# Squares of an RMS norm added in pairs on VectorE ahead of the matmuls that sum them over partitions

## The chip, the cores and the metric

The kernel runs on the 8 cores of one Trainium2 chip. The time of a run is that of its slowest core, in microseconds (us) of the device. A run can fall into a slow state, in which the cores of one die show a lower granted TensorE clock. Unless said otherwise, a time is the median over all runs of a kernel, slow ones included, as the timing reports it; where that matters, the fast runs alone are given beside it.

TensorE (PE) multiplies matrices; its weight loads (PEld) overlap with it (in the second profile of the kernel before, 1898.4 and 875.3 us busy in a span of 2054.5 us). VectorE is DVE, ScalarE is ACT, GpSimd is POOL. The order of instructions on each engine is written down when the program is built.

## The reference, cut to what matters

A decoder step: retention layer, then sliding-window attention layer, each followed by a SwiGLU feed-forward network (FFN), for a prompt (8 sequences of 2048 tokens) and a sample group (128 sequences of 8 tokens). The width is 1024. What the change touches is the norm alone:

```python
def rms_norm(x, g):
    xf = x.astype(jnp.float32)
    y = xf * lax.rsqrt(jnp.mean(xf * xf, axis=-1, keepdims=True) + RMS_EPS)
    return (y * g.astype(jnp.float32)).astype(x.dtype)

for layer in range(DEPTH):          # cut
    hp = rms_norm(xp, norm_mix[layer]);  hs = rms_norm(xs, norm_mix[layer])
    ...                             # retention or attention
    xp = xp + yp;  xs = xs + ys
    xp = xp + swiglu(rms_norm(xp, norm_ffn[layer]), ...)
    xs = xs + swiglu(rms_norm(xs, norm_ffn[layer]), ...)
y_prompt = rms_norm(xp, norm_final);  y_sample = rms_norm(xs, norm_final)
```

## The kernel before: the parts that matter

The activations lie with the 1024 channels on partitions, as `KC = 8` tiles ("columns") of 128 partitions by 512 tokens (prompt) or 128 tokens (sample). The sum over the channels is therefore a sum over partitions and over the eight columns. ScalarE squares each column into one of six buffers `sq`, and TensorE multiplies a matrix of ones by it, eight matmuls that accumulate into one PSUM bank. A core does 25 such norms, 20 of 512 columns (large) and 5 of 128 (sample): 200 matmuls on squares.

```python
def norm_do_sq(self, j):
    kc = j.sq.pop(0)
    s = self.sqi % 6
    while s in self.sqown:
        self.norm_do_mm(self.sqown[s])
    self.sqi += 1
    cx = j.cx
    self.act(self.sq[:, s, :cx.NT], cx.x[:, kc, :cx.NT], AF.Square, [cx.xb[kc]], [self.sqb[s]])
    j.mm.append(s)
    self.sqown[s] = j

def norm_do_mm(self, j):
    ...                                   # cut: takes a PSUM bank
    s = j.mm.pop(0)
    del self.sqown[s]
    NT = j.cx.NT
    self.mm(j.bk[:, :NT], self.cb[:, CB_ONES:CB_ONES + 128], self.sq[:, s, :NT],
            j.nmm == 0, j.nmm == KC - 1, [self.sqb[s], self.cbb], [j.bb])
    j.nmm += 1
    ...                                   # cut: after the eighth, 1/rms on ScalarE
```

When these go into the static order of instructions is decided at build time. After each piece of other work (8 to 16 matmuls, say) the norms get a turn, and a matmul on squares is placed as soon as the scheduler's own clock says that its square is done:

```python
def norm_tick(self):
    t = self.S.t["pe"] + 0.05             # the scheduler's clock for TensorE
    for j in list(self.jobs):
        if j.out:
            self.norm_do_out(j, 2)        # VectorE: two columns of h = x * g / rms
            continue
        for _ in range(4):
            if j.sq and self.S.t_read(j.cx.xb[j.sq[0]]) <= t + 0.5:
                self.norm_do_sq(j)
        while j.mm and self.S.t_read(self.sqb[j.mm[0]]) <= t:
            self.norm_do_mm(j)

def mm(self, out, lhsT, rhs, start, stop, r, w, skip=False):   # its model of a matmul
    k = 0.5 if lhsT.shape[0] <= 64 or self.n(lhsT) <= 64 else 1.0
    self.S.op("pe", ..., dur=k * max(0.1, self.n(out) * 0.00047))
```

The softmax here doesn't subtract the row's maximum and nothing guards it: scores larger than these inputs give would overflow.

Of the kernel before, what the change touches and what calls it, by code (L numbers as in the profile page):

```python
# [9 lines left out]
ALU = mybir.AluOpType  # L10
# [3 lines left out]
KC = 8  # L14
# [373 lines left out]
CB_ONES = 128  # L388
# [120 lines left out]
class Kern:  # L509
# [150 lines left out]
    def norm_begin(self, cx, gi, pool, to_x=False, after=None):  # L660

        j = Ctx()
        j.cx, j.gi, j.pool, j.to_x, j.after = cx, gi, pool, to_x, after
        j.sq, j.mm, j.nmm, j.out, j.bk = [], [], 0, None, None
        self.jobs.append(j)
        cx.job = j
        return j
# [7 lines left out]
# [5 lines that stand above are left out]
        self.sqi += 1  # L680
        cx = j.cx
        self.act(self.sq[:, s, :cx.NT], cx.x[:, kc, :cx.NT], AF.Square, [cx.xb[kc]], [self.sqb[s]])
        j.mm.append(s)
        self.sqown[s] = j

    def norm_do_mm(self, j):
        if j.bk is None:
            pool = j.pool if any(i not in self.held for i in j.pool) else (0, 1, 2, 3)
            j.bk, j.bb, j.hold = self.pb(pool, True)
        s = j.mm.pop(0)  # L690
        del self.sqown[s]
        NT = j.cx.NT
        self.mm(j.bk[:, :NT], self.cb[:, CB_ONES:CB_ONES + 128], self.sq[:, s, :NT], j.nmm == 0, j.nmm == KC - 1, [self.sqb[s], self.cbb], [j.bb])
        j.nmm += 1
        if j.nmm == KC:
            self.nrstd += 1
            j.rstd_ap, (j.rstd_buf,) = self.rstd[self.nrstd % 2]
            for o in list(self.jobs):
                if o.out and o.rstd_buf is j.rstd_buf:
                    self.norm_do_out(o, KC)  # L700
            self.act(j.rstd_ap[:, :NT], j.bk[:, :NT], AF.Ln, [j.bb], [j.rstd_buf], bias=EPS, scale=1.0 / D)
            self.held.discard(j.hold)
            self.act(j.rstd_ap[:, :NT], j.rstd_ap[:, :NT], AF.Exp, [j.rstd_buf], [j.rstd_buf], scale=-0.5)
            j.out = list(range(KC))
# [14 lines left out]
    def norm_tick(self):  # L719

        t = self.S.t["pe"] + 0.05
        for j in list(self.jobs):
            if j.out:
                self.norm_do_out(j, 2)
                continue
            for _ in range(4):
                if j.sq and self.S.t_read(j.cx.xb[j.sq[0]]) <= t + 0.5:
                    self.norm_do_sq(j)
            while j.mm and self.S.t_read(self.sqb[j.mm[0]]) <= t:
                self.norm_do_mm(j)  # L730

    def norm_now(self, cx):

        j = getattr(cx, "job", None)
        if j is None:
            return
        assert j.out or j.nmm + len(j.mm) + len(j.sq) == KC
        while not j.out:
            if j.sq:
                self.norm_do_sq(j)  # L740
                if len(j.mm) < 4 and j.sq:
                    continue
            if j.mm:
                self.norm_do_mm(j)
        self.norm_do_out(j, KC)
# [1139 lines left out]
```

## Time and profile before

| | before |
|---|---|
| time, median of 4 runs | 2054.69 us (2053.55 to 2056.62) |
| span of the profiled cores | 2038.7 to 2058.2 us |
| TensorE busy | 92% |
| VectorE / ScalarE busy | 42% / 36% |
| TensorE waiting for squares | 47.8 us in 39 waits |

The page of the kernel before: part 1 (busy us, share of the span, instructions of each engine), part 4 (the chain that ended last, by engine) and the group of the squares-matmuls in part 5 (busy us, mean ns of one, then the idle time of TensorE just before them).

```profile
PE 1884.1 (92%) x10330; PEld 875.0 (43%) x10514; DVE 870.7 (42%) x1510; ACT 735.0 (36%) x1160; POOL 172.1 (8%) x363
...
PE 75%; DVE 8%; DMA 7%; issue 5%; ACT 4%; DVEq 0%; SPq 0%; POOL 0%; ACTq 0%; another core or an unknown queue 0%; POOLq 0%
...
L576 PE MATMUL ps<-sq,cbt 128*128 128x512 bf16 (+1 forms) x193 | 65.4, 371 | 49.3 <-ACT sq L592 42.9
```

TensorE is what bounds the kernel: it is busy for 92% of the span, and 75% of the chain that ended last lies on it. PE shows 10330 matmuls but 10514 weight loads, so 184 matmul records are missing from this core's trace.

The waits of the kernel before on the same core (engine and what it waited for; us in total, times, longest). One of them, 16.0 us, is at the start of the program, where the first input is loaded.

```profile
PE ps L576 <- ACT sq L592: 47.8, 39, 16.0
```

The timeline of the kernel before in an FFN down-projection (start us, duration us, engine, line, operation, output from inputs, count). Eleven matmuls and one squares-matmul repeat every 2.59 us (2026.04 to 2028.63), so a 128x512 matmul costs 2.59/12 = 0.216 us of the stream, although one alone lasts 0.38 us in the records.

```profile
2023.67 2.54 PE L576 MATMUL ps<-aT_104,wr 128*128 128x512 bf16 x10
2026.04 0.38 PE L576 MATMUL ps<-sq,cbt 128*128 128x512 bf16 x1
2026.26 2.54 PE L576 MATMUL ps<-aT_104,wr 128*128 128x512 bf16 x11
2028.63 0.38 PE L576 MATMUL ps<-sq,cbt 128*128 128x512 bf16 x1
```

And the same view in the second retention stage, where the sample's output projection (4 x 4 matmuls of 128 columns) rides along with the prompt's. In brackets stand TensorE's idle time and what ended it. TensorE's waits for a square stand at the squares-matmuls. (The 0.93 us in the first line stands at an ordinary matmul because the record of the squares-matmul ahead of it is one of the missing ones; its weight load is in the trace, at 1317.48.)

```profile
1317.73 3.61 PE L576 MATMUL ps<-uT_91_134,wr 128*128 128x512 bf16 x16 [0.93 <-ACT sq L592]
1321.18 0.22 PE L576 MATMUL ps<-sq,cbt 128*128 128x128 bf16 x1
1321.24 0.39 PE L576 MATMUL ps<-uTs_121,wr 128*128 128x128 bf16 x4
...
1321.91 0.39 PE L576 MATMUL ps<-uTs_133,wr 128*128 128x128 bf16 x4
1323.12 0.38 PE L576 MATMUL ps<-sq,cbt 128*128 128x512 bf16 x1 [0.83 <-ACT sq L592]
1323.34 3.40 PE L576 MATMUL ps<-uT_91_134,wr 128*128 128x512 bf16 x15
...
1328.73 0.38 PE L576 MATMUL ps<-sq,cbt 128*128 128x512 bf16 x1 [0.83 <-ACT sq L592]
```

### The profile page before, as it was taken

The numbers are of one execution on the slowest core, as the hardware profiler recorded it, in microseconds if no ns is written. First come the engines' busy times: TensorE is split into PE (matmuls) and PEld (weight loads), VectorE is DVE, ScalarE is ACT, GpSimd is POOL, SyncE is SP. The second block draws the span as 40 slices with busy tenths as digits, with TensorE's granted clock in tenths as the row PEclk, the third lists the DMA queues.
The fourth block names the chain that finished last, engine by engine and source line by source line (L and its number), as shares of the span: only waits on it lengthen the run. The fifth ranks groups of instructions, "written<-read, shape, count | busy, mean of one in ns | idle before, by whom it ended". The sixth has DMA issues, their size and how long they took to land.

```text
span 2058.2 us, 30114 instructions; the slowest of 8 cores (2038.7 to 2058.2 us)
## 1 busy us (share of the span) xinstructions
PE 1884.1 (92%) x10330; PEld 875.0 (43%) x10514; DVE 870.7 (42%) x1510; ACT 735.0 (36%) x1160; POOL 172.1 (8%) x363
## 2 busy tenths in 40 slices
PE   4899999999999989899989999899999988899997
PEld 1444444343334334343434444445454532455553
DVE  2454543434335863433555554332222457422224
ACT  2545543321225752122445554221012466310112
POOL 0011111000101000000001111010000000010000
PEclk9899999999999999999999999999999998999999
DMA  9324444897986339888634333554334230134242
GB/s 188 53 40 71 62 72 71 192 192 186 194 183 156 52 63 203 202 204 218 142 113 94 83 72 62 107 82 69 53 57 82 43 62 1 31 66 84 46 73 93
DMA packets 87253, 211.93 MB, mean 103 GB/s; under 512 B 10784, under 2 KB 13728, under 8 KB 84000
## 3 DMA queue, kind: packets, MB, share of 16 engines
q0 software_dynamic: 35952, 114.08, 34.9%
q1 hardware_dynamic: 51152, 95.90, 15.1%
q8 instruction: 88, 1.44, 0.3%
q14 instruction: 61, 0.50, 0.1%
HBM read 277.10 MB, written 48.89 MB: 158 GB/s over the span
## 4 chain that ended last, share of the span: by engine, by line
PE 75%; DVE 8%; DMA 7%; issue 5%; ACT 4%; DVEq 0%; SPq 0%; POOL 0%; ACTq 0%; another core or an unknown queue 0%; POOLq 0%
PE ps L576 74%; DMA wr<-wa 2%; PE ps L581 1%; DVE rt L604 1%; DMA x_62<-xTp 1%; DMA S_1_109<-st_in 1%; DMA S_2_110<-st_in 1%; ACT sq L592 1%; ACT rec_129 L592 1%; DMA x_63<-xTp 1%; DVE rec_130 L607 1%; DMA S_0_108<-st_in 1%; DVE rec_129 L607 1%; DVE h_45 L607 0%; DVE stat L833 0%
## 5 line engine op out<-in xcount | busy, mean ns | idle before, releaser
L576 PE MATMUL ps<-h_44,wr 128*128 128x512 bf16 x1776 | 413.4, 386 | 17.3 <-DMA wr<-wa 4.6
L576 PE MATMUL ps<-h_45,wr 128*128 128x512 bf16 x1784 | 413.4, 383 | 11.4 <-ACT s_105 L592 3.5
L576 PEld LDWEIGHTS ps<-h_44,wr 128*128 128x128 bf16 x1824 | 176.2, 99 | 232.8 <-issue 38.6
L576 PEld LDWEIGHTS ps<-h_45,wr 128*128 128x128 bf16 x1824 | 174.8, 99 | 229.4 <-issue 34.4
L256 POOL DMA_DIRECT2D wr<-w x152 | 80.9, 533 | 1065.6 <-PE ps L576 950.0
L576 PE MATMUL ps<-aT_104,wr 128*128 128x512 bf16 x688 | 157.6, 379 | 2.1 <-DVE aT_137 L604 0.9
L576 PE MATMUL ps<-aT_106,wr 128*128 128x512 bf16 x688 | 158.3, 379 | 1.0 <-issue 0.3
L592 ACT ACTIVATE s_105<-ps 128x512 f32<-128x512 f32 x88 | 52.1, 595 | 299.6 <-PE ps L576 277.2
L604 DVE TENSOR_TENSOR aT_104<-s_105,ps 128x512 bf16<-128x512 f32 x88 | 60.5, 688 | 225.1 <-PE ps L576 172.0
L604 DVE TENSOR_TENSOR aT_106<-s_107,ps 128x512 bf16<-128x512 f32 x88 | 60.5, 688 | 213.0 <-PE ps L576 186.6
L592 ACT ACTIVATE s_107<-ps 128x512 f32<-128x512 f32 x88 | 52.3, 595 | 223.3 <-PE ps L576 208.6
L576 PE MATMUL ps<-wr,h_44 128*128 128x512 bf16 (+1 forms) x564 | 126.0, 369 | 4.5 <-DMA wr<-wa 3.0
L576 PE MATMUL ps<-wr,h_45 128*128 128x512 bf16 (+1 forms) x572 | 123.7, 359 | 0.8 <-issue 0.2
L604 DVE TENSOR_TENSOR x_62<-ps,x_62 128x512 f32<-128x512 f32 x80 | 55.3, 692 | 146.1 <-PE ps L576 145.9
L576 PE MATMUL ps<-sq,cbt 128*128 128x512 bf16 (+1 forms) x193 | 65.4, 371 | 49.3 <-ACT sq L592 42.9
L576 PEld LDWEIGHTS ps<-aT_106,wr 128*128 128x128 bf16 x704 | 67.9, 98 | 82.3 <-issue 2.9
L576 PEld LDWEIGHTS ps<-aT_104,wr 128*128 128x128 bf16 x704 | 67.1, 98 | 82.0 <-issue 4.5
L592 ACT ACTIVATE sq<-x_62 128x512 bf16<-128x512 f32 x80 | 48.0, 623 | 114.4 <-DVE x_62 L604 73.3
L576 PEld LDWEIGHTS ps<-wr,h_44 128*128 128x128 bf16 x576 | 53.2, 100 | 59.9 <-issue 10.2
L576 PEld LDWEIGHTS ps<-wr,h_45 128*128 128x128 bf16 x584 | 52.4, 98 | 51.4 <-issue 1.7
L833 DVE BATCH_NORM_STATS2 stat<-ps 128x6 f32<-128x512 f32 x68 | 47.4, 697 | 57.2 <-PE ps L576 45.0
L592 ACT ACTIVATE u<-on,stat 128x512 bf16<-128x512 f32 x64 | 46.1, 721 | 69.7 <-POOL stat L836 63.1
(292 smaller groups left out, 2238.2 us busy)
## 6 DMA issues: line engine op xcount, KB each, us to landing
wr<-w POOLq DMA_DIRECT2D x88, 512.0 KB, 7.4
wr<-wa POOLq DMA_DIRECT2D x24, 1024.0 KB, 10.4
wr<-w POOLq DMA_DIRECT2D x64, 352.0 KB, 6.9
wr<-wo POOLq DMA_DIRECT2D x16, 512.0 KB, 8.3
S_0_108<-st_in SPq DMA_DIRECT2D x16, 512.0 KB, 6.7
S_1_109<-st_in SPq DMA_DIRECT2D x16, 512.0 KB, 6.6
S_2_110<-st_in SPq DMA_DIRECT2D x16, 512.0 KB, 7.2
S_3_111<-st_in SPq DMA_DIRECT2D x16, 512.0 KB, 6.4
```

The source lines that it names most:

```text
L256: self.S.op("pool", (lambda o_, i_: (lambda e: e.dma_start(out=o_, in_=i_)))(dst, src), self.gate.get(self.next, ()), [b], dsem=f"w{self.n ...
L576: self.S.op("pe", lambda e: e.matmul(out, lhsT, rhs, start=start, stop=stop, skip_group_check=skip), r, w, dur=k * max(0.1, self.n(out) * ...
L581: self.S.op("pe", lambda e: e.transpose(out, in_, ident), list(r) + [self.cbb], w, dur=0.1)
L592: self.S.op("act", lambda e: e.activation(out=out, in_=in_, func=func, bias=bias, scale=scale), r, w, dur=dur)
L604: self.dve(lambda e: e.tensor_tensor(out=out, in0=in0, in1=in1, op=op), out, r, w, (in0, in1))
L607: self.dve(lambda e: e.scalar_tensor_tensor(out=out, in0=in0, scalar=scalar, in1=in1, op0=op0, op1=op1), out, r, w, (in0,))
L833: S.op("dve", lambda e: e.bn_stats(out=st[:, 0:6], in_=ob), [obb], [sb], dur=0.7)
```

## The change

Its intent: add the squares in pairs on VectorE, so that TensorE sums fewer tiles. Columns 0+1, 2+3 and 4+5 are added; 6 and 7 stay single, so that the end of a norm is not later by an addition. A norm then takes 5 matmuls in place of 8: 125 instead of 200 over the program, 60 of 512 columns and 15 of 128 columns fewer, for 75 additions on VectorE. The diff, without the assertion:

```diff
@@ norm_do_sq
         self.act(self.sq[:, s, :cx.NT], cx.x[:, kc, :cx.NT], AF.Square, [cx.xb[kc]], [self.sqb[s]])
-        j.mm.append(s)
-        self.sqown[s] = j
+        if j.half is not None:
+            a = j.half
+            j.half = None
+            NT = cx.NT
+            self.tt(self.sq[:, a, :NT], self.sq[:, a, :NT], self.sq[:, s, :NT], ALU.add, [self.sqb[a], self.sqb[s]], [self.sqb[a]])
+            j.mm.append((a, 2))
+        else:
+            self.sqown[s] = j
+            if kc % 2 == 0 and kc < KC - 2:
+                j.half = s
+            else:
+                j.mm.append((s, 1))
@@ norm_do_mm
-        s = j.mm.pop(0)
+        if not j.mm:
+            j.mm.append((j.half, 1))
+            j.half = None
+        s, wt = j.mm.pop(0)
...
-        self.mm(..., j.nmm == 0, j.nmm == KC - 1, ...)
-        j.nmm += 1
+        self.mm(..., j.nmm == 0, j.nmm + wt == KC, ...)
+        j.nmm += wt
@@ norm_tick
-            while j.mm and self.S.t_read(self.sqb[j.mm[0]]) <= t:
+            while j.mm and self.S.t_read(self.sqb[j.mm[0][0]]) <= t:
```

The addition enters VectorE's queue together with the second square, so it can stand there unfinished ahead of other work. And the matmul of a pair can only be placed after both squares and the addition.

More of the change, by code (lines that the diff above doesn't have):

```diff
@@ L663, in norm_begin @@
         j.cx, j.gi, j.pool, j.to_x, j.after = cx, gi, pool, to_x, after
-        j.sq, j.mm, j.nmm, j.out, j.bk = [], [], 0, None, None
+        j.sq, j.mm, j.nmm, j.out, j.bk, j.half = [], [], 0, None, None, None
         self.jobs.append(j)
@@ L689, in norm_do_mm @@
             j.bk, j.bb, j.hold = self.pb(pool, True)
-        s = j.mm.pop(0)
+        if not j.mm:
+            j.mm.append((j.half, 1))
+            j.half = None
+        s, wt = j.mm.pop(0)
         del self.sqown[s]
         NT = j.cx.NT
-        self.mm(j.bk[:, :NT], self.cb[:, CB_ONES:CB_ONES + 128], self.sq[:, s, :NT], j.nmm == 0, j.nmm == KC - 1, [self.sqb[s], self.cbb], [j.bb])
-        j.nmm += 1
+        self.mm(j.bk[:, :NT], self.cb[:, CB_ONES:CB_ONES + 128], self.sq[:, s, :NT], j.nmm == 0, j.nmm + wt == KC, [self.sqb[s], self.cbb], [j.bb])
+        j.nmm += wt
         if j.nmm == KC:
@@ L736, in norm_now @@
             return
-        assert j.out or j.nmm + len(j.mm) + len(j.sq) == KC
+        assert j.out or j.nmm + sum(w for _, w in j.mm) + (j.half is not None) + len(j.sq) == KC
         while not j.out:
```

## The prediction

> **What bounds the kernel now.** TensorE. The page gives PE 92% busy of a 2058.2 us span (DVE 42%, ACT 36%), and the chain that ended last lies on PE for 75%. In FFN stretches the timeline shows PE as an unbroken stream: down-projections of 11 matmuls with one squares-matmul after each repeat every 2.59 us, so a 128x512 matmul costs 2.59/12 = 0.216 us of stream, not the 0.37-0.39 us of the pipelined means. The Trainium skill ("TensorE: Matmul & The Clock Gate", Back-to-back issue gap) states 216 ns for an isolated warm gap at N=512; this trace agrees.
>
> **What the change removes.** 25 norms (20 of 512 columns, 5 of 128), each with 8 ones-matmuls, become 5 matmuls each: 60 matmuls of 128x512 and 15 of 128x128 leave PE. By stream cost that is 60 x 0.216 = 13.0 us, plus 15 x about 0.06 = 0.9 us (11 matmuls of 128x128 take about 0.67 us between starts). ACT keeps all its squares.
>
> **What it adds.** 75 bf16 additions on DVE. The like operation in the trace (Qz, 128x512 bf16 from bf16) takes 0.42-0.43 us, against 0.69 us for f32; at 128 columns I estimate 0.22 us. Together about 29 us on DVE, which rises from 871 to about 900 us (44%). The skill ("VectorE: DVE Perf Modes", What auto-detection actually checks) lets a two-source op of packed 16-bit tensors take its double rate; the Qz time agrees.
>
> **How much is on the critical path.** Four large norms at the starts of the two retention stages gain little: PE waits there for data (16-55 us and 1041-1050 us in the timeline: x landing, then the squares), and the first two lie wholly in that wait. The other 16 or 17 sit in the PE stream, where each gives 3 x 0.216 = 0.65 us: 10.4 to 11 us. DVE has slack of about 1.9 us between x updates in the FFN tails, so a 0.43 us addition fits, and the last two squares stay single, so the end of a norm is not later. In the sample norms PE waits for nearly every square (waits of 0.5 to 1.3 us at 1586-1620, 1764-1775, 2017-2050 us; all waits of PE on squares sum to 47.8 us): three of eight waits disappear, but the pair's wait grows by the addition, sometimes behind two 0.7 us DVE outputs. I count about zero. Given back: an addition in DVE's in-order queue waits for its square and can hold up the next eviction or score mask by up to about 1 us in the retention tail and after attention, and the final tail, where DVE is nearly unbroken from 2042 to 2053 us, grows by about 0.7 us. Together 1 to 2 us.
>
> **Predicted time.** 2054 - 11 + 1.5 = about 2044.5 us, range 2037 to 2051. Faster by over 2%: 0.01; within 2%: 0.98; slower by over 2%: 0.01.
>
> **What would show it.** Squares-matmuls 200 -> 125 (weight loads count all); PE busy down 12 to 16 us; DVE busy up 26 to 31 us, additions of 0.40-0.45 us; ACT unchanged; intervals of the FFN-down stream 2.59 -> 2.37 us at the three places per norm without a matmul; waits of PE on squares about as long as before, now partly on DVE additions; FFN stretches without norms unchanged.
>
> **What would make it wrong.** DVE additions held behind slow squares delaying bank releases (then PE waits on DVE x updates rise and the gain shrinks below 5 us); the static order shifting elsewhere, since the scheduler places work by its own clock; a lower granted clock in the PE gaps; or sample norms losing or winning more than 2 us.

## The result, and the profile after

| | before | after |
|---|---|---|
| time, median of 4 runs | 2054.69 us | 2043.57 us (2040.58 to 2093.77) |
| ratio of the fast runs | | 0.994, 95% interval 0.992 to 0.996 |
| span of the profiled cores | 2038.7 to 2058.2 us | 2026.1 to 2040.2 us |

The ratio is the mean time of the changed kernel's fast runs over that of the other's fast runs of the same rounds, so it is not quite the ratio of the medians. The run at 2093.77 us is slow: the cores of die 1 had a clock of 0.943 to 0.948 against 0.978 to 0.980; without it the median is 2041.28 us. The granted clock is no rival explanation: in both profiles the median core of each die had 0.980. Both kernels give the correct result.

The page of the changed kernel, the same parts:

```profile
PE 1889.8 (93%) x10439; PEld 868.6 (43%) x10439; DVE 893.6 (44%) x1585; ACT 734.9 (36%) x1160; POOL 171.5 (8%) x363
...
L576 PE MATMUL ps<-sq,cbt 128*128 128x512 bf16 (+1 forms) x125 | 40.9, 369 | 46.6 <-DVE sq L604 38.6
```

There are 125 squares-matmuls now. PE seems to have risen, from 1884.1 to 1889.8 us, but this trace has all its records. A second profile of the kernel before (the last run below) has them on its slowest core too:

```profile
PE 1898.4 (92%) x10514; PEld 875.3 (43%) x10514; DVE 870.6 (42%) x1510; ACT 734.9 (36%) x1160; POOL 171.8 (8%) x363
```

To set aside the differences between cores, I summed TensorE's busy time in the traces over the cores that have all records (six of eight in each of these), with the rest of the span as idle time:

| mean of six cores, us | TensorE busy | not busy | of it ahead of squares-matmuls |
|---|---|---|---|
| before, two profiles | 1895.6, 1896.3 | 153.7, 150.1 | 51.3, 50.7 |
| after, two profiles | 1883.6, 1883.9 | 152.6, 152.2 | 48.6, 49.0 |

Busy time fell by 12.2 us and idle time stayed, within its spread. In this book-keeping the fall looks like the removed matmuls and nothing else. It isn't proof of that. Busy time also moves while the number of matmuls stays: the kernels of the experiments below with the same 125 squares-matmuls have between 1877.8 us (e5) and 1887.6 us (e10), and e4, with all 200, has 1892.2 us (means of six cores). One likely reason, not tested, is that a matmul's record of 0.38 us covers up to 0.16 us more than its 0.216 us of stream, and so hides that much of a wait behind it. And that idle time stayed is a sum, as the timeline shows.

The groups of the additions in the changed kernel, each shape apart. They cost 24.8 + 3.3 = 28.1 us; VectorE's busy time rose by less, from 870.7 to 893.6 us, because the records of neighbouring operations overlap (in the timeline below, by about 0.08 us each, as 736.40 + 1.41 against 737.73).

```profile
L604 DVE TENSOR_TENSOR sq<-sq 128x512 bf16<-128x512 bf16 x60 | 24.8, 419 | 24.4 <-ACT sq L592 24.3
L604 DVE TENSOR_TENSOR sq<-sq 128x128 bf16<-128x128 bf16 x15 | 3.3, 221 | 9.3 <-ACT sq L592 9.3
```

Its waits: TensorE now waits for sums, fewer times, and VectorE waits for the squares that it is to add.

```profile
PE ps L576 <- DVE sq L604: 38.6, 23, 17.1
DVE sq L604 <- ACT sq L592: 33.6, 25, 6.6
PE ps L576 <- ACT sq L592: 4.4, 10, 1.2
```

The FFN stream of the changed kernel: between two squares-matmuls lie two down-projections back to back, 4.96 us (1989.80 to 1994.76) for what took 2 x 2.59 us.

```profile
1989.80 0.38 PE L576 MATMUL ps<-sq,cbt 128*128 128x512 bf16 x1
1990.01 4.91 PE L576 MATMUL ps<-aT_106,wr 128*128 128x512 bf16 x22
1994.76 0.38 PE L576 MATMUL ps<-sq,cbt 128*128 128x512 bf16 x1
```

The second retention stage of the changed kernel. The waits of 0.8 us behind the sample's matmuls are gone: one matmul of a pair and one more come in one place with no wait, and a piece takes 4.6 us (1299.16 to 1303.77) in place of 5.6 us (1317.73 to 1323.34 in the kernel before).

```profile
1299.16 3.61 PE L576 MATMUL ps<-uT_91_134,wr 128*128 128x512 bf16 x16
1302.61 0.43 PE L576 MATMUL ps<-sq,cbt 128*128 128x512 bf16 x2
...
1303.77 3.62 PE L576 MATMUL ps<-uT_91_134,wr 128*128 128x512 bf16 x16
...
1308.33 3.61 PE L576 MATMUL ps<-uT_91_134,wr 128*128 128x512 bf16 x16
1311.78 0.43 PE L576 MATMUL ps<-sq,cbt 128*128 128x512 bf16 x2
```

The end of the first attention stage, before and after. Before, a squares-matmul follows each piece of eight and waits for nothing:

```profile
744.50 0.38 PE L576 MATMUL ps<-sq,cbt 128*128 128x512 bf16 x1
744.71 1.89 PE L576 MATMUL ps<-qo_124,wr 128*128 128x512 bf16 x8
746.44 0.38 PE L576 MATMUL ps<-sq,cbt 128*128 128x512 bf16 x1
```

After, the matmul of each pair waits 0.9 us for its sum. On VectorE the addition stands behind two outputs `h` of another norm (1.41 us for two):

```profile
736.40 1.41 DVE L607 SCALAR_TENSOR_TENSOR h_44<-x_62,spt,rstd_57 128x512 bf16<-128x512 f32 x2
737.73 0.42 DVE L604 TENSOR_TENSOR sq<-sq 128x512 bf16<-128x512 bf16 x1
738.29 0.38 PE L576 MATMUL ps<-sq,cbt 128*128 128x512 bf16 x1 [0.93 <-DVE sq L604]
738.50 3.62 PE L576 MATMUL ps<-qo_124,wr 128*128 128x512 bf16 x16
743.05 0.59 PE L576 MATMUL ps<-sq,cbt 128*128 128x512 bf16 x2 [0.93 <-DVE sq L604]
```

So the change took waits away in one stage and made waits in another. For each stage I measured the time between the same two matmuls (not on squares) in the traces, as the median of the eight cores. The stages that are bound by DMA transfers are left out; they differ by up to 4 us between the two profiles of the kernel before. In the rows of the attention ends and of the sample norm the values shift by up to 0.9 us with the choice of the two matmuls.

```
change of a stage's length, us, against the second profile of before
stage (us of that profile)                before(1st)  after(two profiles)
1st retention, last part (253-329)           -0.01      -1.62  -1.62
end of 1st attention (710-753)               -0.20      +2.67  +1.91
2nd retention, last part (1251-1292)         -0.00      -1.62  -1.62
2nd retention with sample (1292-1342)        -0.00      -5.94  -5.94
end of an FFN, sample norm (1569-1607)       -0.56      -2.28  -1.46
end of 2nd attention (1729-1778)             -2.49      -0.36  +0.36
last FFN (1778-2006)                         -0.00      -1.21  -1.21
```

The largest gain, 5.9 us in some 50 us, is not what three matmuls fewer per norm give there. One stage left out belongs beside it: around 551 to 597 us, where transfers of the state come in, the median core is 3.6 us shorter in both profiles of the change, and the two profiles of the kernel before differ by 0.1 us. (Single cores spread widely there: 43 to 50 us before, 43 to 47 us after.)

### The profile page after: what moved, and what is told of

It reads as the page before. It is cut to its first block, busy times and chain, and to the rows that moved or that the text cites. A ratio compares the mean times of both kernels' runs of the same rounds, so it can differ in the third digit from the quotient of the medians.

```text
span 2040.2 us, 30119 instructions; the slowest of 8 cores (2026.1 to 2040.2 us)
## 1 busy us (share of the span) xinstructions
PE 1889.8 (93%) x10439; PEld 868.6 (43%) x10439; DVE 893.6 (44%) x1585; ACT 734.9 (36%) x1160; POOL 171.5 (8%) x363
## 4 chain that ended last, share of the span: by engine, by line
PE 77%; DVE 9%; DMA 6%; issue 4%; ACT 3%; DVEq 0%; SPq 0%; ACTq 0%; POOL 0%; POOLq 0%
PE ps L576 75%; PE ps L581 1%; DVE rt L604 1%; DMA x_62<-xTp 1%; DMA S_0_108<-st_in 1%; DMA S_2_110<-st_in 1%; DMA S_1_109<-st_in 1%; DMA x_63<-xTp 1%; DVE rec_130 L607 1%; ACT rec_129 L592 1%; DMA wr<-wa 1%; DVE h_45 L607 1%; ACT sq L592 1%; DVE rec_129 L607 1%; DVE stat L846 0%
## 5 line engine op out<-in xcount | busy, mean ns | idle before, releaser
L576 PE MATMUL ps<-h_45,wr 128*128 128x512 bf16 x1824 | 421.8, 385 | 10.3 <-ACT s_105 L592 3.6
L576 PE MATMUL ps<-h_44,wr 128*128 128x512 bf16 x1824 | 419.7, 386 | 8.6 <-ACT rstd_57 L592 3.9
L576 PE MATMUL ps<-aT_104,wr 128*128 128x512 bf16 x704 | 157.7, 379 | 0.9 <-DVE aT_137 L604 0.7
L576 PE MATMUL ps<-aT_106,wr 128*128 128x512 bf16 x704 | 157.5, 379 | 0.0
L576 PE MATMUL ps<-sq,cbt 128*128 128x512 bf16 (+1 forms) x125 | 40.9, 369 | 46.6 <-DVE sq L604 38.6
```

The costliest lines, as they stand in the source:

```text
L576: self.S.op("pe", lambda e: e.matmul(out, lhsT, rhs, start=start, stop=stop, skip_group_check=skip), r, w, dur=k * max(0.1, self.n(out) * ...
```

## The experiments

Twelve runs were made (e1 to e4, e5 to e8, e9 to e12), each on one chip with its own runs of the kernel before (medians 2055.08, 2053.75 and 2053.92 us). One run each of e1, e2, e10, e11 and e12 fell in the slow state.

| run | what it is | median us | ratio (95% interval) |
|---|---|---|---|
| e1_after_again | the change, unaltered | 2043.25 | 0.9945 (0.9932 to 0.9959) |
| e2_double | the change, pair matmuls twice | 2051.99 | 0.9987 (0.9968 to 1.0005) |
| e3_tiny_adds | the change, additions of 2 columns | 2036.89 | 0.9913 (0.9900 to 0.9926) |
| e4_before_defer | before, squares-matmuls 0.9 us later | 2047.09 | 0.9964 (0.9949 to 0.9979) |
| e5_late_adds | pairs, additions late, matmuls 2.0 us later | 2025.36 | 0.9847 (0.9811 to 0.9883) |
| e6_before_defer2 | before, squares-matmuls 2.0 us later | 2041.71 | 0.9940 (0.9903 to 0.9978) |
| e7_only_large | the change in the large norms alone | 2045.58 | 0.9947 (0.9913 to 0.9981) |
| e8_late_six | as e5, six columns summed on VectorE | 2035.47 | 0.9907 (0.9872 to 0.9941) |
| e9_defer_only | the change, matmuls 2.0 us later | 2024.94 | 0.9862 (0.9845 to 0.9879) |
| e10_late_adds_only | the change, additions late | 2047.49 | 0.9962 (0.9944 to 0.9980) |
| e11_late_double | e5 with pair matmuls twice | 2034.37 | 0.9904 (0.9887 to 0.9921) |
| e12_before_again | before, one look | 2055.55 (fast run) | |

Means of the fast runs alone are 2043.1 (e1), 2052.0 (e2), 2036.9 (e3), 2025.1 (e5), 2025.3 (e9), 2046.4 (e10) and 2033.9 us (e11). The differences drawn below from the medians agree with theirs within about 1 us.

My theory after the result: the removed matmuls give their stream time, the additions give back more than I had thought, and the later places of the matmuls take waits away. The rivals: the matmuls alone explain it all; or the additions are free, and the gain is smaller because TensorE would have waited anyhow.

### e1_after_again

No edit; it repeats the result on the chip on which the next three ran.

> The changed kernel itself, unaltered, as the yardstick for its neighbours on this chip. Every theory: 10 to 13 us faster than before (ratio about 0.994).

Measured: 2043.25 us, 0.9945. The result stands.

### e2_double

Each matmul of a pair is issued twice, with the scheduler's clock put back, so that the order is that of the change and TensorE has 200 squares-matmuls again. The sums are wrong.

```diff
-        self.mm(..., j.nmm == 0, j.nmm + wt == KC, ...)
+        for rep in range(wt):
+            t0 = self.S.t["pe"]
+            self.mm(..., j.nmm + rep == 0, j.nmm + rep == KC - 1, ...)
+            if rep:      # the second costs the scheduler's clock nothing
+                self.S.t["pe"] = t0
+                self.S.fin[("e", "pe"), self.S.cnt["pe"]] = t0
```

> Changed kernel, same order on every engine and same additions, but each of the three matmuls on a pair is issued twice, so TensorE has its 8 squares-matmuls per norm back (result wrong on purpose). Theory 1, the gain is the stream time of the removed matmuls: 11 us slower than the changed kernel, about level with before. Rival, the gain is the changed order and the fewer waits on squares: at most 5 us slower than the changed kernel. By stage I expect the retention tail of the second half to stay about 5 us shorter than before even so, because waits on squares are gone there, and the two ends of the attention layers to stay longer than before.

Measured: 2051.99 us, 8.7 us above the change (2051.99 - 2043.25). That lies between theory 1 (11 us) and the rival (at most 5 us). So the 75 matmuls are worth about 8.7 us of the time, with a wide interval (that of the two ratios allows some 4 us either way; by the medians of the fast runs it is 7.4 us). Over the six complete cores TensorE's busy time rose by 12.7 us (1896.4 against 1883.7, the mean of the change's two profiles) and its idle time fell by 6.9 us (145.5 against 152.4). That suggests that a part of the matmuls ran in time that was idle otherwise, but it does not show it: the profiled execution, at 2048.09 us, is the fastest of this kernel's runs. Where the traces repeat to 0.02 us, each added matmul costs its full stream time: the last part of the first retention has three more of them than in the change and is 0.65 us longer (74.86 against 74.21 us). The kernel is still 2.7 us below before by the means' ratio, but the interval reaches 1.0005, so that remainder is not shown by the times. In the second retention stage, however, the trace is plain; the timeline of this kernel there:

```profile
1302.91 3.61 PE L576 MATMUL ps<-uT,wr 128*128 128x512 bf16 x16
1306.36 0.71 PE L576 MATMUL ps<-sq,cbt 128*128 128x512 bf16 x4
1306.90 1.06 PE L576 MATMUL ps<-uTs,wr 128*128 128x128 bf16 x16
```

Four squares-matmuls in one place, no wait, and the stage is still 5.40 us shorter than before. The 5.9 us gained there are therefore not the matmuls' stream time (0.5 us of them is), but the waits, which the changed order took away.

### e3_tiny_adds

The additions work on 2 columns instead of 512 or 128; the order is that of the change, the result is wrong.

```diff
-            self.tt(self.sq[:, a, :NT], self.sq[:, a, :NT], self.sq[:, s, :NT], ALU.add, ...)
+            o2, i2 = self.sq[:, a, :2], self.sq[:, s, :2]
+            self.S.op("dve", lambda e: e.tensor_tensor(out=o2, in0=o2, in1=i2, op=ALU.add), ...,
+                      dur=0.09 + NT * 0.00058)     # as modelled before
```

> Changed kernel, same order, but each addition covers 2 columns in place of 512 or 128 (result wrong on purpose), so VectorE loses about 25 of the 29 us. If the additions are free, the same time as the changed kernel within 1 us. If they are given back where TensorE waits on them (six pairs at the two attention ends, 0.9 us each), 2 to 4 us faster. If they hold up VectorE's other work at large, 6 us or more faster.

Measured: 2036.89 us, 6.4 us below the change. The group of the additions in this kernel:

```profile
L688 DVE TENSOR_TENSOR sq<-sq 128x2 bf16<-128x2 bf16 x75 | 11.2, 154 | 35.7 <-ACT sq L592 35.6
```

Taking 28.1 - 11.2 = 16.9 us of work off VectorE, an engine that is busy for 44%, was worth 6.4 us (with the two intervals, between 3 and 10). The expectation's third case began at 6 us, its second ended at 4: the interval does not part them. The waits for squares stay nearly as they were (46.0 us ahead of squares-matmuls against 48.8). At the ends of the attention stages the trace shows where a part of it lies: +1.10 and -2.40 us against before, where the change has +2.3 and 0.0 (means of two profiles; the second of these stages also differs by 2.5 us between the two profiles of before).

### e4_before_defer

The kernel before with one edit; there are no additions and no pairs.

```diff
-            while j.mm and self.S.t_read(self.sqb[j.mm[0]]) <= t:
+            while j.mm and self.S.t_read(self.sqb[j.mm[0]]) + 0.9 <= t:
```

> Kernel before, all 8 matmuls single, no additions; only the scheduler puts a squares-matmul into TensorE's queue 0.9 us later by its own clock than it did, which in the second retention tail is one piece later. Theory 1 alone: same as before within 2 us. If waits on squares are worth something by themselves: 4 to 6 us faster than before, and the second retention tail 5 us shorter.

Measured: 2047.09 us, 8 us below before. Waits ahead of squares-matmuls fell from 51.0 to 38.2 us (mean of six cores). Merely placing the 200 matmuls later is worth about two thirds of the whole change. In the trace all other matmuls of TensorE keep the order of the kernel before, so on that engine only the squares-matmuls changed places. But in the second retention stage only 1.15 us of the 5.94 appeared; 0.9 us was too little there.

### e5_late_adds

Pairs as in the change, but the addition is given to VectorE only when the scheduler's clock says that both squares are done, and the matmul is placed 2.0 us after its sum.

```diff
...                 # cut: the new norm_do_add, and the list j.wait of additions not yet given out
+            while j.wait and max(self.S.t_read(self.sqb[i]) for i in j.wait[0][:2]) <= t:
+                self.norm_do_add(j)
-            while j.mm and self.S.t_read(self.sqb[j.mm[0][0]]) <= t:
+            while j.mm and self.S.t_read(self.sqb[j.mm[0][0]]) + 2.0 <= t:
```

> Pairs as in the change and a right result, but the scheduler emits an addition only once both squares are done by its clock, and a squares-matmul only 2 us after its operand is. If what the additions cost (6 us between the tiny and the full ones) is queueing, behind squares that aren't ready or ahead of a waiting matmul, it comes back: 4 to 8 us faster than the changed kernel, so about 2035 to 2039. If it is VectorE time as such: no faster than the changed kernel.

Measured: 2025.36 us, more than expected: 28 us below before, 18 us below the change. Two edits are mixed here; e9 and e10 part them.

### e6_before_defer2

As e4 with 2.0 us.

> Kernel before with single squares, squares-matmuls emitted 2 us later by the scheduler's clock (0.9 us in the run before, which left the 0.8 us waits in the second retention tail). If those waits are what the change removed there, that tail (51 us) gets 5 us shorter as in the changed kernel and the whole lies 10 to 13 us below before, level with the change without one addition. If the tail's gain needs the pairs: as the 0.9 us run, 8 us below before.

Measured: 2041.71 us, level with the change (2043.25) without one addition. The waits ahead of squares-matmuls fell to 30.6 us. The second retention stage is 8.22 us shorter than before, so the gain of that stage comes from the place of the matmuls alone. The end of the first attention, though, is 10.31 us longer. Its timeline shows a wait that is not for squares: a matmul of the next retention stage was placed ahead of the work that fills the time before its state `S` is ready.

```profile
750.64 0.60 PE L576 MATMUL ps<-rv,KZ 32*128 32x512 bf16 x3
756.37 0.58 PE L576 MATMUL ps<-rv,KZ 32*128 32x512 bf16 x1 [5.13 <-DVE S L607]
```

Because of this accident of the order (and some 6 us more around 551 to 597 us, where a square stands on ScalarE behind a copy of the state that waits 11.5 us for its transfer, and TensorE waits 6.9 us for the square) the difference between e6 and e9 is not the worth of the pairs.

### e7_only_large

Pairs in the norms of 512 columns alone.

```diff
-            if kc % 2 == 0 and kc < KC - 2:
+            if kc % 2 == 0 and kc < KC - 2 and cx.NT == TT:
```

> The change in the 20 norms of 512 columns alone; the 5 sample norms of 128 columns stay single. My forecast counted the sample norms as about zero: same time as the changed kernel within 2 us. If their fewer waits pay: 3 us or more slower than the changed kernel.

Measured: 2045.58 us, 0.9947 against 0.9945 for the change. The sample norms are worth nothing that the times show. Stage by stage it is less even: in the second retention stage this kernel gains 2.53 us where the change gains 5.94.

### e8_late_six

As e5, but columns 0 to 5 are all added into one tile: 3 matmuls in a norm, 125 additions. The way in which the six `sq` buffers are handed out had to change with it (cut below), so this is not one edit alone.

```diff
-        if kc == 0 or kc in (2, 4):
+        if kc == 0:
             j.half = s
         elif kc < KC - 2:
-            j.wait.append((j.half, s, kc % 2 == 1))      # the pair is complete
+            j.wait.append((j.half, s, kc == 5))          # the six are complete
...
-            j.mm.append((a, 2))
+            j.mm.append((a, 6))
```

> As the late additions, but six columns are summed on VectorE, so 3 squares-matmuls per norm in place of 5. If removed stream time pays as the doubled run showed (75 matmuls, 8 to 9 us), 50 fewer give 5 to 6 us below the late-additions run. If VectorE's further 50 additions give it back: no gain over that run, or a loss.

Measured: 2035.47 us, 10 us above e5, with 50 squares-matmuls fewer. Idle time rose from 142.5 to 153.2 us (mean of six cores), most of it ahead of squares-matmuls (32.5 to 42.1). The end of the first attention alone is 7.65 us longer than in e5 (+7.80 against +0.15). That the further additions caused this, and not the buffers, is not shown. TensorE waits there for the outputs `h` on VectorE:

```profile
734.64 0.38 PE L576 MATMUL ps<-h,wr 128*128 128x512 bf16 x1 [1.55 <-DVE h L607]
736.53 0.38 PE L576 MATMUL ps<-h,wr 128*128 128x512 bf16 x1 [0.86 <-DVE h L607]
740.30 2.57 PE L576 MATMUL ps<-h,wr 128*128 128x512 bf16 x4 [2.73 <-DVE h L607]
```

### e9_defer_only

The change, with the one edit to the matmuls; the additions stay where the change puts them.

```diff
-            while j.mm and self.S.t_read(self.sqb[j.mm[0][0]]) <= t:
+            while j.mm and self.S.t_read(self.sqb[j.mm[0][0]]) + 2.0 <= t:
```

> The changed kernel with one edit: the matmuls over partitions come into the order 2.0 us later; the additions stay where the change puts them, handed to VectorE right behind the second square of a pair. Question: whether the late additions or the late matmuls made the late-additions kernel (2025.4 us) 18 us faster than the changed kernel. Theory A (two waits of equal weight: TensorE waiting for a pair's sum, and VectorE held up at its in-order queue by an addition whose square is not done): the late matmuls alone give about half, 2032 to 2038 us. Theory B (TensorE's waits on squares are nearly all of it; the additions cost nothing by their place): within 3 us of the late-additions kernel. Theory C (the additions' place is nearly all of it): within 4 us of the changed kernel, 2040 to 2045 us.

Measured: 2024.94 us (four runs), level with e5. The one edit gives the whole of that gain (theory B). It is one edit of the scheduler, but it moved more than the squares-matmuls: in the trace other matmuls of TensorE (among them `rv,KZ`, `S0f,Qz` and `cbt,us`) changed places in six stretches as well. Stage by stage about 11 of the 18 us fall in stretches where no other matmul moved (the second retention, the sample norms and the end of the second attention above all); for the rest the two causes are not parted. The group of the squares-matmuls in this kernel:

```profile
L576 PE MATMUL ps<-sq,cbt 128*128 128x512 bf16 (+1 forms) x125 | 39.8, 364 | 30.9 <-DVE sq L604 24.2
```

The waits on the same core:

```profile
DVE sq L604 <- ACT sq L592: 37.7, 30, 7.1
PE ps L576 <- DVE sq L604: 24.2, 6, 17.5
PE ps L576 <- ACT sq L592: 1.7, 2, 1.3
```

Without the one long wait at the start (17.5 us), TensorE waits 24.2 - 17.5 = 6.7 us for sums, where the changed kernel waits 38.6 - 17.1 = 21.5 us. VectorE still waits for squares, as long as in the change (37.7 against 33.6 us): that costs nothing that can be seen here. The end of the first attention in this kernel, to be read against that of the change above: the matmuls of the pairs stand between the same pieces of work, each later than in the change, and wait for nothing.

```profile
730.26 1.89 PE L576 MATMUL ps<-qo,wr 128*128 128x512 bf16 x8
731.99 0.38 PE L576 MATMUL ps<-sq,cbt 128*128 128x512 bf16 x1
732.21 3.62 PE L576 MATMUL ps<-qo,wr 128*128 128x512 bf16 x16
735.66 0.38 PE L576 MATMUL ps<-sq,cbt 128*128 128x512 bf16 x1
```

Against before, this stage is now +0.22 us, the end of the second attention -4.42 us, and the second retention stage -8.45 us.

### e10_late_adds_only

The counterpart: late additions as in e5, without the 2.0 us.

> The counterpart: the additions are handed over only when the scheduler's clock says that both squares are done, and the matmul follows as soon as its sum counts as done, without the 2.0 us. Theory A: about the other half, 2033 to 2039 us. Theory B: within 4 us of the changed kernel, about 2040 to 2045 us. Theory C: within 3 us of the late-additions kernel. If the two single edits together are worth much less than 18 us, the late-additions kernel owes part of its gain to the two working together: a late addition without a later matmul is waited for by TensorE.

Measured: 2047.49 us, 4.2 us above the change. Late additions alone are worth nothing; the interval of its ratio (0.9944 to 0.9980) meets that of the change (0.9932 to 0.9959). TensorE's waits ahead of squares-matmuls stay at 48.0 us. With the matmuls placed late the additions' place makes no difference either (e5 against e9). So the 18 us were not won by moving the additions. It does not follow that their place costs nothing: here a later addition also makes the sum later, and the two effects can cancel.

### e11_late_double

e5 with the matmuls of pairs doubled as in e2.

> The late-additions kernel with each matmul of a pair issued twice, 200 in all as before the change (wrong on purpose: the pairs are counted twice). In the changed kernel the same doubling cost 8.7 us, less than the 10.4 to 11 us that the prediction forecast for the 75 removed matmuls. Theory A (a part of the matmuls then ran in time in which TensorE waited for squares anyhow): with those waits reduced, the doubling costs more, 10 to 13 us. Theory B (the matmuls are worth less than their stream time for another reason, such as that TensorE is not what ends the DMA-bound stages): it costs 7 to 9 us again. Both expect TensorE's busy time in the profile to rise by 60 times 0.216 plus 15 times about 0.06 us, some 13 to 15 us.

Measured: 2034.37 us. That is 9.0 us above e5 by the medians and 9.4 us above e9; by the ratios, 0.0057 x 2054 = 11.7 us above e5 and 8.6 us above e9. The two theories (10 to 13, 7 to 9) are not told apart. Busy time rose by 11.5 us over e5 (1889.3 against 1877.8), less than the 13 to 15 that both expected. In the last part of the first retention three doubled matmuls cost 0.65 us again (74.43 against 73.78 us in e5): no part of them is hidden there, in either order.

### e12_before_again

The kernel before, one look, for a second profile. One of its two runs was slow (2259.77 us); the profiled one is fast.

> The kernel before, unaltered, for one more profile: the first lacks 184 of 10514 matmul records, so its TensorE busy time can't be compared with the changed kernel's. If all records are there, it should show about 1898 to 1903 us of TensorE busy time (the deferred kernel before shows 1900.7 with all of them), 12 to 16 above the changed kernel's 1886 to 1890, and 47 to 55 us of TensorE waits on squares again. The stages bound by transfers differ from the first profile by 2 to 5 us if what was read there is noise.

Measured: 1898.4 us of TensorE busy time with all 10514 matmuls. The expectation holds. The transfers' stages differ from the first profile by up to 4.1 us (190.4 us in one and 194.5 us in the other), so a few us there explain nothing.

## Why the prediction was right, and where not

**The total: right, in part by luck.** 2044.5 us forecast, 2043.57 us measured (2041.28 us over the fast runs). The forecast was 11 us for the matmuls less 1.5 us for the additions. The experiments give 8.7 us less 6.4 us, and a third term that the forecast did not have, the moved waits, fills the gap of some 9 us (if the terms are taken to add). The prediction named a shift of the static order among the things that would make it wrong, but put no number on it.

**"PE busy down 12 to 16 us": right.** 12.2 us on the six complete cores, and 12.7 us come back with the 75 matmuls in e2, which keeps the order. The first profile of before could not show it, for want of 184 records. The stream cost of 0.216 us held: two FFN pieces with one squares-matmul less took 4.96 us, as 2.59 + 2.37 forecast. The Trainium skill ("TensorE: Matmul & The Clock Gate", Back-to-back issue gap) has this 216 ns as the gap of an isolated matmul; the trace has the same number, but as the steady spacing of a stream, for which that section states less (see the last section).

**"10.4 to 11 us" on the critical path: a little high, or right.** The doubling gives 8.7 us in the change and 8.6 to 11.7 us in the late order. The intervals do not separate this from 10.4. In the steady stages of the traces a matmul is worth its 0.216 us.

**"Given back ... together 1 to 2 us": wrong in size.** Shrinking the additions won 6.4 us, with 17 of their 28 us taken away. I had compared an addition of 0.43 us with VectorE's slack in the FFN tails, and counted holds of up to about 1 us in the retention tail and after attention, 1 to 2 us in all. At the ends of attention an addition stands in line with `h` outputs of 0.7 us each, and three waits of about 0.9 us for sums come up in each of the two ends. Through which waits the whole 6.4 us go is seen only in part.

**"Waits of PE on squares about as long as before": the sum was right (51.0 and 48.8 us), the reason was not.** I took these waits as given, so that the change could only swap their cause. In truth they depend on where the static order puts the matmul. The change moved it, and the second retention stage became 5.9 us shorter, of which 5.4 remained when all the matmuls were issued; at the ends of attention new waits of 0.9 us for sums came up. The first was not forecast, the second only as holds of up to about 1 us. Moving the matmuls alone, without any pair, was worth 8 us (0.9 us later). With the change, 2.0 us later was worth another 17 (by the ratios) to 18 us (by the medians), some 7 of them in stretches where other matmuls moved too.

Why the matmuls on squares came too early is argued, not shown: the scheduler's clock gives every matmul of 128 columns at least 0.1 us, so 16 of them 1.6 us. In the trace of the kernel before, twelve of them start within 0.67 us (1321.24 to 1321.91), so 16 take about 0.9 us. The clock thus counts some 0.7 us there that do not pass, and TensorE waits 0.8 us. It also gives a matmul of 512 columns 0.24 us, where the stream takes 0.216: 0.4 us more in the 16 of a piece. The two together, an estimate of 1.1 us, would fit that 0.9 us later was too little there (e4) and 2.0 us enough (e6, e9). No run corrected the model itself.

**"Sample norms about zero": right in the total.** With the large norms alone the ratio is 0.9947, against 0.9945.

**"DVE busy up 26 to 31 us": 22.9 us.** The additions last what I had estimated (0.42 and 0.22 us; 28.1 us against 29), but the records overlap. The double rate for 16-bit operands of two sources, which the skill states ("VectorE: DVE Perf Modes", What auto-detection actually checks), is in line with 419 ns for 512 columns in bf16 beside 0.69 us for f32. It is not a like pair, though: the f32 operations of this kernel that take 0.69 us read one operand from PSUM.

**What stays open.** The parts do not add up exactly: 8.7 us for the matmuls less 6.4 us for the additions leaves some 9 us of the measured 11.3 (e1's, by the ratio) to the changed order, if the terms are taken to add. The times show that only for the sum: e2's remainder of 2.7 us has an interval that touches zero. The traces show the waits that went and came.

## What to carry to other kernels

When a bound engine waits in a static order, the wait belongs to the place of the instruction, not only to the work: before removing matmuls, try to issue those that wait a piece later. Here one constant in the scheduler, on top of the change, gave more (18 us) than the change did (11 us), and the two together give 2024.94 us, 1.4% under the kernel before. Such a constant can move other work as well: compare the whole order, not only what you meant to move. Additions on an engine that is busy for less than half the time were not free here (6.4 us when they were shrunk), and the kernel with more of them (six columns summed) was slower.

When busy times are compared, first see that the counts of records agree with those of the weight loads, and do not read a busy time as a count of matmuls.

## What the Trainium skill lacked or had wrong

- "TensorE: Matmul & The Clock Gate", Back-to-back issue gap, states about 131 ns as the sustained spacing of 128x512 matmuls that alternate with weight loads, and calls the 216 ns of the isolated gap too high for that. Here every matmul has its weight load, and the steady spacing is 216 ns (2.59 us for 12).
- The same section states about 81 ns for 128 columns in such a stream, against 56 ns of the isolated formula. Here twelve of them with their loads take 0.67 us (56 ns each).
- "Perfetto Trace Analysis" does not advise to compare the count of matmul records with that of weight loads before busy times are compared: 10330 against 10514 on one core of before. That this shows as 14 us less TensorE busy time (1884.1 against 1898.4 in the second profile, on another core) cost me the check of my own prediction at first.
- No page that I read deals with matmuls placed too early in a static order: in the second retention 0.72 to 0.83 us of idle time for each here, and 18 us in all for the one constant that issues them 2.0 us later.
